# Issuing the loads of modulation weights that go with interleaved steps from GpSimd's queue

## The chip, the cores and the metric

The kernel runs on one core of a Trainium2 chip. The metric is the device time of one launch in microseconds; lower is better. The engines of a core work side by side, each through its own queue in order: TensorE (PE) for matrix products, VectorE (DVE), ScalarE (ACT) and GpSimd (POOL) for the rest, and SyncE (SP), which here only issues loads and stores.

## The reference, cut to what matters

Two stacks of blocks run over one sequence of 512 tokens of width 1024, in 32-bit floats. The change touches the second stack only. There, each of two layers is modulated by a vector `c`:

```
c_act = silu(c)
for i in range(2):
    mod = c_act @ ada_w[i] + ada_b[i]          # [1024] x [1024, 6144]
    sh1, sc1, g1, sh2, sc2, g2 = split(mod, 6)
    h = rmsnorm(x, g[i, 0]) * (1 + sc1) + sh1
    y = mlstm(h) if i == 0 else sgu(h)         # sgu: the gated mixer
    x = x + g1 * rmsnorm(y, g[i, 1])
    h = rmsnorm(x, g[i, 2]) * (1 + sc2) + sh2
    y = square(relu(h @ w1[i])) @ w2[i]        # the feed-forward part, hidden width 4096
    x = x + g2 * rmsnorm(y, g[i, 3])
return x
```

`ada_w` is `ada_w_2` in the kernel. Each of the twelve parts of the two products `c_act @ ada_w[i]` needs 4 MB of weights and next to no arithmetic.

## The kernel before

All large products run on TensorE as three products of split operands: a weight piece of 256 rows and 512 columns (512 KB) is loaded by SyncE (L210 in `w_piece`, L391 in `seven`, which forms products of blocks with fewer multiplications), ScalarE writes its high part (L191) and VectorE the rest (L192); TensorE then runs the products of lines 287 to 289. The raw piece and both parts lie in slots of one pool, `mid`, which are taken again in the order in which they come free. In the mixer there are eleven such slots for weights.

The modulation products run on VectorE. A part of 1024 columns is summed in 16 steps, eight row blocks times two halves of 512 columns. A load of 128 x 512 values (256 KB, L562) brings the weights into one of two buffers, taken in turn (`ada_in`); the step multiplies them by one column of `c_act` and adds them to an accumulator (L571 for the first two steps, L573 after that). A load is put in the program one step ahead: step i issues load i+1. Load i+1 writes the buffer that step i-1 has read.

Where `ada_sum` has no `then`, all 16 steps stand in the program in one place: three parts in the first stack's first mixer and two in the mlstm. Where it has one, the steps go to a list, `ada_steps`, and `dense` takes `ada_rate` of them (two or three) ahead of each weight piece. That is so for the feed-forward part of layer 0 (its own part 5, and parts 0 and 1 of layer 1), for the gated mixer `sgu` (parts 3, 4 and 2 of layer 1; the last with an empty function) and for the feed-forward part of layer 1 (part 5).

The order in which each engine gets its instructions is planned ahead, by readiness and program order, and is fixed when the kernel runs; so a step can stand earlier or later than the program puts it. The planner also sets the waits.

GpSimd has other work: the differences of weight blocks in `seven` (lines 411, 415, 420 and 425), the addition of a bias in the gated mixer (L1558), sums of blocks (lines 363 and 367), and the reciprocal root of every norm (L480). It issues no load.

Of the kernel before, what the change touches and what calls it, by code (L numbers as in the profile page):

```python
# [16 lines left out]
P = 128  # L17
# [13 lines left out]
def kernel(ctx: ExitStack, tc: tile.TileContext, inp: dict, out: bass.AP):  # L31
    nc = tc.nc
    V, S, G, T = nc.vector, nc.scalar, nc.gpsimd, nc.tensor
# [520 lines left out]
    def ada_sum(l, part, then=None):  # L554


        ts = []

        def load(i):
            ts.append(ada_in[0].next())  # L560
            c0 = part * D + (i % 2) * 512
            nc.sync.dma_start(ts[i], inp["ada_w_2"][l, i // 2 * P : (i // 2 + 1) * P, c0 : c0 + 512])  # L562

        def step(i):
            if i == 0:
                load(0)
            if i < 2 * KD - 1:
                load(i + 1)
            a, t, ck = ada_acc[i % 2], ts[i], c_act[:, i // 2 : i // 2 + 1]
            if i < 2:  # L570
                V.tensor_scalar(a, t, ck, None, op0=mult)  # L571
            else:
                V.scalar_tensor_tensor(a, t, ck, a, op0=mult, op1=add)  # L573

        steps = [lambda i=i: step(i) for i in range(2 * KD)]
        if then:
            ada_steps.extend((*steps, lambda: None, then, lambda: None, lambda: None))
        else:
            for f in steps:
                f()  # L580
# [1065 lines left out]
```

## Time and profile before

| | |
|---|---|
| median of 3 runs | 2264.4 us (2262.87 to 2268.69) |
| the profiled execution's own time | 2268.93 us |
| its span, first to last instruction | 2266.9 us |
| TensorE busy | 2215.9 us, 98% |
| VectorE busy | 1471.9 us, 65% |
| ScalarE busy | 975.1 us, 43% |
| GpSimd busy | 239.2 us, 11% |
| loads of modulation weights | 192, 256 KB each |

The rows further down come from one execution. Times are microseconds from the start of the span, unless a row says ns. SPq is SyncE's queue, POOL is GpSimd. The second stack's feed-forward part of layer 0 runs from about 1230 to 1590, the gated mixer from about 1590 to 1900, the last feed-forward part after that. A wait is put down to what came last of all that an instruction waited for.

### The profile page before, as it was taken

The numbers are of one execution on the slowest core, as the hardware profiler recorded it, in microseconds if no ns is written. First come the engines' busy times: TensorE is split into PE (matmuls) and PEld (weight loads), VectorE is DVE, ScalarE is ACT, GpSimd is POOL, SyncE is SP. The second block draws the span as 40 slices with busy tenths as digits, with TensorE's granted clock in tenths as the row PEclk, the third lists the DMA queues.
The fourth block names the chain that finished last, engine by engine and source line by source line (L and its number), as shares of the span: only waits on it lengthen the run. The fifth ranks groups of instructions, "written<-read, shape, count | busy, mean of one in ns | idle before, by whom it ended". The sixth has DMA issues, their size and how long they took to land.

```text
span 2266.9 us, 29330 instructions
## 1 busy us (share of the span) xinstructions
PE 2215.9 (98%) x11112; PEld 1820.6 (80%) x11112; DVE 1471.9 (65%) x2610; ACT 975.1 (43%) x1784; POOL 239.2 (11%) x209
## 2 busy tenths in 40 slices
PE   8999999999999999999999999999999899999998
PEld 6787888787778777887777888988777787898996
DVE  5665755844995857843647847867667748655765
ACT  4333344424344544343444534525434335443543
POOL 0000000100000000000211131221002200131130
PEclk9999999999999999999999999999999999999999
DMA  5343424222222124223414435352344434323322
GB/s 166 120 125 108 151 85 122 98 71 66 84 75 75 38 88 142 91 71 115 141 61 131 154 111 167 103 177 87 113 154 149 141 133 139 104 85 101 119 93 77
DMA packets 158062, 251.16 MB, mean 111 GB/s; under 512 B 13785, under 2 KB 59057, under 8 KB 157921
## 3 DMA queue, kind: packets, MB, share of 16 engines
q1 hardware_dynamic: 157920, 249.29, 34.8%
q8 instruction: 87, 1.43, 0.3%
q14 instruction: 55, 0.44, 0.1%
HBM read 247.15 MB, written 2.10 MB: 110 GB/s over the span
## 4 chain that ended last, share of the span: by engine, by line
PE 76%; DVE 10%; DMA 7%; ACT 3%; issue 3%; POOL 1%; SPq 0%; DVEq 0%; POOLq 0%; ACTq 0%
PE bank L287 23%; PE bank L288 23%; PE bank L289 23%; DMA small<-in_ada_w_dram 4%; DVE mid L192 3%; DVE small L573 2%; PE bank L1109 2%; PE bank L294 1%; ACT mid L191 1%; POOL tiny_c L480 1%; PE bank L1124 1%; PE bank L1308 1%; PE bank L1293 1%; DMA mid<-in_b_w_in_dram 1%; DVE x_res L642 0%
## 5 line engine op out<-in xcount | busy, mean ns | idle before, releaser
L192 DVE TENSOR_TENSOR mid<-mid,mid 128x512 fp32r<-128x512 f32 (+2 forms) x530 | 512.9, 989 | 443.1 <-ACT mid L191 278.1
L191 ACT CAST mid<-mid 128x512 fp32r<-128x512 f32 (+2 forms) x530 | 419.6, 818 | 761.0 <-DMA mid<-in_ffn_w_dram 138.6
L287 PE MATMUL bank<-mid,mid 128*128 128x512 f32 (+1 forms) x1320 | 492.8, 373 | 7.5 <-ACT small L1567 4.4
L288 PE MATMUL bank<-mid,mid 128*128 128x512 f32 (+1 forms) x1320 | 489.8, 371 | 1.5 <-DVE mid L192 1.5
L289 PE MATMUL bank<-mid,mid 128*128 128x512 f32 (+1 forms) x1320 | 489.2, 371 | 0.0
L287 PE MATMUL bank<-xt_hi,mid 128*128 128x512 f32 (+1 forms) x1216 | 426.9, 352 | 11.7 <-ACT small L1567 5.8
L289 PE MATMUL bank<-xt_hi,mid 128*128 128x512 f32 (+1 forms) x1216 | 425.1, 350 | 1.3 <-DVE mid L192 1.3
L288 PE MATMUL bank<-xt_lo,mid 128*128 128x512 f32 (+1 forms) x1216 | 424.7, 349 | 0.0
L287 PEld LDWEIGHTS bank<-mid,mid 128*128 128x128 f32 x1320 | 248.9, 189 | 56.3 <-ACT small L1567 4.8
L288 PEld LDWEIGHTS bank<-mid,mid 128*128 128x128 f32 x1320 | 248.7, 188 | 46.0 <-DVE mid L192 2.1
L289 PEld LDWEIGHTS bank<-mid,mid 128*128 128x128 f32 x1320 | 248.7, 188 | 45.3
L287 PEld LDWEIGHTS bank<-xt_hi,mid 128*128 128x128 f32 x1216 | 229.4, 189 | 48.3 <-ACT small L1567 6.7
L289 PEld LDWEIGHTS bank<-xt_hi,mid 128*128 128x128 f32 x1216 | 229.6, 189 | 32.7 <-DVE mid L192 1.5
L288 PEld LDWEIGHTS bank<-xt_lo,mid 128*128 128x128 f32 x1216 | 229.8, 189 | 31.9 <-issue 1.3
L287 PE MATMUL bank<-mid,xt_hi 128*128 128x512 f32 (+1 forms) x640 | 252.7, 395 | 0.0
L288 PE MATMUL bank<-mid,xt_hi 128*128 128x512 f32 (+1 forms) x640 | 250.2, 391 | 0.0
L289 PE MATMUL bank<-mid,xt_lo 128*128 128x512 f32 (+1 forms) x640 | 250.1, 391 | 0.0
L573 DVE SCALAR_TENSOR_TENSOR small<-small,c_act,small 128x512 f32<-128x512 f32 x168 | 132.5, 804 | 78.6 <-DMA small<-in_ada_w_dram 77.9
L289 PEld LDWEIGHTS bank<-mid,xt_lo 128*128 128x128 f32 x640 | 120.5, 188 | 26.6
L288 PEld LDWEIGHTS bank<-mid,xt_hi 128*128 128x128 f32 x640 | 120.6, 188 | 25.5 <-DVE mid L192 0.3
L287 PEld LDWEIGHTS bank<-mid,xt_hi 128*128 128x128 f32 x640 | 120.7, 189 | 24.9
L480 POOL TENSOR_TENSOR tiny_c<-tiny_c,minus_half 128x1 f32<-128x1 f32 (+1 forms) x68 | 52.3, 773 | 747.5 <-DVE tiny_c L494 375.5
(297 smaller groups left out, 2305.0 us busy)
## 6 DMA issues: line engine op xcount, KB each, us to landing
mid<-in_ffn_w_dram SPq DMA_DIRECT2D x128, 512.0 KB, 3.7
small<-in_ada_w_dram SPq DMA_DIRECT2D x192, 256.0 KB, 2.9
mid<-in_dsa_w_in_dram SPq DMA_DIRECT2D x36, 512.0 KB, 3.5
mid<-in_gla_w_in_dram SPq DMA_DIRECT2D x32, 512.0 KB, 4.4
mid<-in_b_w_in_dram SPq DMA_DIRECT2D x32, 512.0 KB, 3.6
mid<-in_a_w_in_dram SPq DMA_DIRECT2D x24, 512.0 KB, 3.8
mid<-in_gla_w_in_dram SPq DMA_DIRECT2D x32, 256.0 KB, 3.0
mid<-in_gla_w_out_dram SPq DMA_DIRECT2D x16, 512.0 KB, 3.7
```

The source lines that it names most:

```text
L191: S.copy(hi, src)
L192: V.tensor_sub(lo, src, hi.bitcast(F32))
L287: T.matmul(o, lhsT=lh, rhs=rh, start=start, stop=False)
L288: T.matmul(o, lhsT=lh, rhs=rl, start=False, stop=False)
L289: turns.passed(o, T.matmul(o, lhsT=ll, rhs=rh, start=False, stop=stop))
L294: i = T.transpose(b[:, blk(c)], src, ident)
L480: G.tensor_tensor(r, v, minus_half[:, 0:m], op=ALU.pow)
L573: V.scalar_tensor_tensor(a, t, ck, a, op0=mult, op1=add)
L1109: T.matmul(b[:, :n], lhsT=QT[tb][:, blk(c)], rhs=KT[:, :n], start=True, stop=True)
L1124: T.transpose(b[:, blk(c)], es[c][:, blk(j)], ident)
L1293: T.matmul(sb[:, :n], lhsT=KT[pr, c // 2, blk(j)], rhs=QT[pr, c // 2, j * P :], start=True, stop=True)
L1308: T.matmul(nb[i // 2][:, (i % 2) * 129 : (i % 2) * 129 + 129], lhsT=Dm[j][:, blk(i - j)], rhs=vv[j][:, c, :], start=j == 0, stop=j == i)
```

## The change

The loads of those sums whose steps go to the list are issued by GpSimd (`G` is `nc.gpsimd`); the others are issued by SyncE as before. Buffers, steps and arithmetic are the same.

```
         def load(i):
             ts.append(ada_in[0].next())
             c0 = part * D + (i % 2) * 512
-            nc.sync.dma_start(ts[i], inp["ada_w_2"][l, i // 2 * P : (i // 2 + 1) * P, c0 : c0 + 512])
+            (G if then else nc.sync).dma_start(ts[i], inp["ada_w_2"][l, i // 2 * P : (i // 2 + 1) * P, c0 : c0 + 512])
```

## Rows read from the trace of the kernel before

**Rows 1.** The page, first part: busy us, share of the span, instructions.
```profile
PE 2215.9 (98%) x11112; PEld 1820.6 (80%) x11112; DVE 1471.9 (65%) x2610; ACT 975.1 (43%) x1784; POOL 239.2 (11%) x209
```
**Rows 2.** Stretches: length, busy us of each engine (instructions), clock, DMA share, GB/s.
```profile
1385.00:1430.00 45.00, 43.38 (x207) 35.76 (x207) 29.09 (x35) 9.43 (x10) 9.97 (x4) 1.00 0.54 174
...
1670.00:1800.00 130.00, 118.88 (x545) 96.96 (x544) 97.82 (x133) 47.15 (x65) 29.07 (x22) 0.95 0.52 164
...
1930.00:2267.00 337.00, 328.65 (x1936) 288.32 (x1935) 203.71 (x208) 145.12 (x200) 67.47 (x29) 1.00 0.30 97
```
**Rows 3.** The chain by line: 1200-1240, 1240-1300, 1385-1430, 1470-1510, 1670-1800, 1870-1930.
```profile
by line: DMA small<-in_ada_w_dram 20.8%; DVE small L573 15.9%; DVE x_res L642 9.1%; issue 7.5%; POOL tiny_c L480 7.5%; DVE mid L192 5.7%; DVE small L1372 5.4%; DVE xt_lo L192 4.6%; ACT junk L486 4.2%; DVE small L520 3.0%; DVE small L519 3.0
...
by line: DVE mid L192 18.3%; issue 16.2%; DMA small<-in_ada_w_dram 9.0%; PE bank L289 6.3%; PE bank L287 6.2%; PE bank L288 5.5%; DVE small L573 4.1%; POOL tiny_c L480 3.2%; PE bank L294 2.9%; DVE x_res L642 2.6%; DVE small L617 2.3%; DVE m
...
by line: DMA small<-in_ada_w_dram 49.6%; DVE small L573 19.2%; DVE mid L192 6.2%; issue 4.9%; PE bank L287 4.2%; DVE small L1455 4.2%; PE bank L289 3.4%; PE bank L288 3.4%; DVE tiny_c L589 2.7%; SPq L391 1.0%; DVE small L571 0.9%; SPq L562 
...
by line: DMA small<-in_ada_w_dram 27.1%; PE bank L287 18.6%; PE bank L288 17.5%; PE bank L289 17.4%; DVE mid L192 7.4%; DVE small L573 5.5%; issue 2.6%; DVE small L1455 1.5%; DVE tiny_c L589 1.5%; DVE small L571 1.0%; DVE tiny_c L599 0.2%; 
...
by line: DMA small<-in_ada_w_dram 18.8%; PE bank L287 12.7%; PE bank L288 11.9%; PE bank L289 11.6%; DMA mid<-in_b_w_in_dram 7.4%; DVE mid L192 7.3%; DVE small L573 5.5%; issue 3.3%; DMA mid<-in_b_w_out_dram 2.9%; ACT mid L191 2.8%; DMA sma
...
by line: DMA small<-in_ada_w_dram 13.8%; DVE mid L192 10.7%; DVE small L573 10.6%; issue 9.7%; POOL tiny_c L480 8.6%; DVE small L1369 6.6%; DVE x_res L642 6.2%; DVE xt_lo L192 4.4%; DVE small L627 3.6%; PE bank L287 3.4%; DVE small L520 3.0
```
**Rows 4.** Pieces of the chain, 1385 to 1425: start, us, what.
```profile
1387.53 4.93 DMA small<-in_ada_w_dram
...
1392.55 0.76 DVE small L573
1393.33 2.85 DMA small<-in_ada_w_dram
...
1409.92 4.88 DMA small<-in_ada_w_dram
```
**Rows 5.** VectorE's waits, 1200 to 1930: us in total, times, longest.
```profile
DVE small L573 <- DMA small<-in_ada_w_dram: 63.6, 43, 4.6
```
**Rows 6.** SyncE's timeline in the mixer: start, us of the run, issues.
```profile
1714.35 2.45 SPq L562 DMA_DIRECT2D small<-in_ada_w_dram  x2
...
1748.55 1.62 SPq L562 DMA_DIRECT2D small<-in_ada_w_dram  x2
...
1781.29 4.16 SPq L562 DMA_DIRECT2D small<-in_ada_w_dram  x3
```
**Rows 7.** Weight pieces in the chain, 1670 to 1800.
```profile
1716.89 3.86 DMA mid<-in_b_w_in_dram
...
1750.26 5.76 DMA mid<-in_b_w_in_dram
...
1785.50 3.71 DMA mid<-in_b_w_out_dram
```
**Rows 8.** TensorE's waits, 1670 to 1800.
```profile
PE bank L287 <- ACT small L1567: 10.2, 3, 4.4
```
**Rows 9.** VectorE's timeline, 1730 to 1800: two steps.
```profile
1752.31 0.75 DVE L573 SCALAR_TENSOR_TENSOR small<-small,c_act,small 128x512 f32<-128x512 f32 x1 [2.49 <-DMA small<-in_ada_w_dram]
...
1786.14 0.75 DVE L573 SCALAR_TENSOR_TENSOR small<-small,c_act,small 128x512 f32<-128x512 f32 x1
```
**Rows 10.** The changed line, 1200 to 1930: ns of an issue min/median/max; landing.
```profile
L562 SPq DMA_DIRECT2D small<-in_ada_w_dram x110: 327/328/456, 1202.0 to 1912.2; - x110
...
DMA to landing us min/median/max: 2.7/2.9/6.3
```
**Rows 11.** GpSimd's groups, 1200 to 1930: busy us, mean ns, idle before.
```profile
L1558 POOL TENSOR_TENSOR mid<-mid,small 128x512 f32<-128x512 f32 x16 | 28.7, 1814 | 72.7 <-DVE mid L1557 72.7
...
L425 POOL TENSOR_TENSOR mid<-mid,mid 128x1024 f32<-128x1024 f32 x6 | 14.5, 2410 | 17.9 <-issue 17.9
```
**Rows 12.** GpSimd's timeline, 1690 to 1730: one instruction, idle before it in brackets.
```profile
1695.94 1.06 POOL L501 TENSOR_SCALAR tiny_c<-tiny_c 128x1 f32<-128x1 f32 x1 [85.06 <-DVE tiny_c L500]
```
**Rows 13.** The step's line, 1200 to 1930: ns min/median/max, first and last start.
```profile
L573 DVE SCALAR_TENSOR_TENSOR small<-small,c_act,small x98: 681/751/2889, 1205.2 to 1920.1; 128x512 f32<-128x512 f32 x98
```

More of the change, by code (lines that the diff above doesn't have):

```diff
@@ L561, in load @@
             c0 = part * D + (i % 2) * 512
-            nc.sync.dma_start(ts[i], inp["ada_w_2"][l, i // 2 * P : (i // 2 + 1) * P, c0 : c0 + 512])
+            (G if then else nc.sync).dma_start(ts[i], inp["ada_w_2"][l, i // 2 * P : (i // 2 + 1) * P, c0 : c0 + 512])
         def step(i):
```

## The prediction

> **What bounds the kernel now.** The page was read first: TensorE is busy for nearly the whole span [rows 1], so a change that only moves loads can win no more than TensorE's gaps in the stretches where those loads run, and what it can lose has no such limit. The stretches come next [rows 2]. From 1385 to 1430 us (the first down-projection of the first feed-forward part) TensorE is busy 43.38 of 45 us; from 1670 to 1800 (the gated mixer) 118.88 of 130, at a granted clock of 0.95 of full speed, which lies between its two levels of 1.2 and 2.4 GHz; from 1930 to the end no load of the changed line is left. The 11.1 us of gap and the lower clock (5 in 100 of 118.88, 5.9 us) are what there is to win in the mixer.
>
> The chain of work that ended last says what fills the gaps [rows 3]. In six stretches a large share of it is the loading of modulation weights: 20.8% of 40 us, 9.0% of 60, 49.6% of 45, 27.1% of 40, 18.8% of 130 and 13.8% of 60, which is 8.3 + 5.4 + 22.3 + 10.8 + 24.4 + 8.3 = 79.5 us. The pieces of the chain show the pattern [rows 4]: a load of 2.9 to 4.9 us, a VectorE step of 0.76 us, the next load within 0.1 us. There are 3, 2, 6, 3, 7 and 3 such pieces in the stretches, 24 in all, 3.31 us each. The reason is the ring of two buffers: load i+1 writes the buffer that step i-1 reads, so it is issued when that step ends, and VectorE, whose queue is in order, stands at step i+1 until it has landed. VectorE waited so 43 times for 63.6 us between 1200 and 1930 [rows 5]. SyncE is not late for these loads: it issues them the moment the step ends. It is late for the weight pieces queued behind them [rows 6].
>
> **The change part by part.** *How many.* The sums with a step after them are those of the first feed-forward part (parts 5 of layer 0, 0 and 1 of layer 1), of the mixer (3, 4, 2; the empty lambda of part 2 counts too) and of the second feed-forward part (5): seven sums of 16 loads, 112 of 192. All 24 trips of the chain are theirs. The loads, the buffers and the steps stay; the queue changes, and with it who stands behind whom.
>
> *Removed: weight pieces standing behind modulation loads in SyncE's queue.* In the mixer the chain has three weight pieces [rows 7]; each was issued within 0.1 us of the end of a run of modulation loads [rows 6]: 1714.35 + 2.45 = 1716.80 against 1716.89, 1748.55 + 1.62 = 1750.17 against 1750.26, 1781.29 + 4.16 = 1785.45 against 1785.50. TensorE's three waits for the gelu that is queued behind their splits cost 10.2 us [rows 8]. Issued earlier, the second piece would gain at most until VectorE's own last step there, 1752.31 + 0.75 = 1753.06 against a landing at 1756.02: 3.0 us; the third 1786.89 against 1789.21: 2.3 us [rows 7, 9]; the first gets a third of the 10.2, 3.4. That is 8.7; I take 7, as a piece also needs a free slot. Bounds: 0, and 10.2 + 5.9 of clock = 16.
>
> *Moved: the issue itself.* SyncE's issue takes 0.33 us and the load lands 2.9 us after its start (median) [rows 10]. The trace has no load issued by GpSimd. From below it costs 0.33, as now; from above 2.4, as a GpSimd operation on 1024 elements [rows 11]. The nearest row is a GpSimd instruction on one element per partition that comes after idle, 1.06 us [rows 12]: almost nothing to move, so it is the engine's own cost. I take 1.0, which is 0.67 more for each trip: 24 x 0.67 = 16 us. Nothing hides it, because VectorE already waits in each of the 24. Bounds: 0 and 24 x 2.07 = 50. The Trainium skill speaks against the change here: "DMA: Bandwidth & Descriptors", Latency and other measured facts, has the first byte about 0.4 us later from GpSimd than from SyncE. By that estimate the term would be some 10 us instead of 16; no run here shows it yet.
>
> *Own queue.* The long trips, 4.93 and 4.88 us [rows 4], have a weight piece in the same queue ahead of them. If all 24 took the shortest, 2.7 [rows 10], that would be 79.5 - 64.8 = 15 us less. Both queues still share the same engines, so I take a third, 5 us (bounds 0 and 15).
>
> *Past GpSimd's queue.* Between 1385 and 1430 GpSimd has 10 us of other work [rows 2], four differences of 2.4 us each and more for the next product [rows 11]; a load whose buffer comes free during one stands for the rest of it, and a difference behind a load that waits for VectorE stands too, and with it the split that ScalarE makes of it. In the mixer the additions (1.8 us, 16 of them [rows 11]) wait for VectorE, and loads stand behind those. At the part boundaries the reciprocal root of a norm can stand behind an issue of 1.0 us. Worst in a down-projection would be all 10 us; two of them and the mixer's 16 x 1.8 = 29 give a bound of 49; below it is 0, where the planned order keeps them apart. I take 6: half a difference twice in each of two down-projections (4.8), and one issue ahead of one root (1.0).
>
> *Sum:* 16 + 6 - 7 - 5 = +10 us on the profiled execution's own 2268.93: 2278.9. That execution is 4.5 us above the median of the runs shown, so as a median 2274.4; I say 2274.
>
> **The rivals.** *The loads come no later (faster).* If GpSimd's issue costs no more than SyncE's, the 16 fall away and the conflicts shrink to about 2: 2 - 7 - 5 = -10, a median of 2254. For it speaks that SyncE's queue is really held up [rows 6] and that GpSimd idles most of the span [rows 1]; against it that its smallest instruction takes three times an issue of SyncE [rows 10, 12]. It decides from 0.25 us: (7 + 5 - 6)/24 is the added time for a trip at which the sum is nil. The Trainium skill's fit in "DMA: Bandwidth & Descriptors", Anatomy of one DMA, 2.0 us and the bytes over 436 GB/s, gives 2.6 us for these 256 KB from GpSimd, an estimate below the 2.9 of the row; by it each trip would shrink by 0.3 and the result be on this side, some 17 us below the profiled execution (24 x 0.3 = 7, and the 10 above).
>
> *The order is planned anew (same).* The program's order on each engine is made ahead, and steps were pulled forward over other work (the second feed-forward part's are over by 1930). A plan that knows the loads to be later puts splits in front of the steps, and the longer trips fall where VectorE had idle time: 97.82 of 130 us are busy in the mixer [rows 2]. Then +16 becomes about +8, and the sum +2: 2266. Against it: VectorE waited for loads 43 times under the present plan too.
>
> *GpSimd is held up while VectorE works (much slower).* A VectorE step took 2.889 us at the longest where 0.751 is usual [rows 13], beside GpSimd's differences. If issuing a load suffers in the same way, each trip gains about 2 us: 48 + 6 - 12 = +42, a median of 2306. Against it: an issue need not read a tile. The Trainium skill, "SBUF — State Buffer", the section SBUF: two separate sides, has GpSimd shut out from writing descriptors while VectorE runs in its two-port mode; by that rule the time would come out here, if the steps ran in that mode; no run here shows yet whether they do.
>
> **How the numbers follow.** 0.3% of the median is 6.8 us, about what a measurement of this kernel can tell from none. The forecast, +3 to +22, gets 0.42, of which 0.09 lies within 0.3%. The much slower case gets 0.10, the new plan 0.22, the faster case 0.26, of which 0.04 lies within 0.3%. Slower: 0.33 + 0.10 = 0.43. Same: 0.09 + 0.22 + 0.04 = 0.35. Faster: 0.22. The range has to reach into the cases of both signs: its low end is the faster case's 2254 (0.12 lies below), its high end 2298, where an added 1.6 us for each trip would stand (0.08 above). The forecast's own range is 2267 to 2286.
>
> **What would show it.** In the changed kernel's profile a second queue carries 29 MB (112 x 256 KB); the issue rows give the time to landing, which I expect at 3.3 to 3.9 us against 2.9; VectorE's waits for these loads grow from 63.6 us towards 90; SyncE's weight pieces in the mixer leave earlier and TensorE's wait for the gelu shrinks; in the down-projections TensorE's gap grows from 1.6 us to several. Wrong would be the whole of it if the landing time stayed at 2.9 or less, or if VectorE's waits grew while TensorE's gaps did not.

## The result and the profile after

The changed kernel takes 2302.45 us (median of 4 runs, 2297.8 to 2307.21), the kernel before 2266.06 in the same session: ratio 1.0156 (95% interval 1.0135 to 1.0178), 36 us slower. The prediction was 2274, with a range from 2254 to 2298. The direction was right, the size too small.

The profiled execution of the changed kernel took 2307.21 us, the longest of its four (TensorE's granted clock was 0.86 of full speed between 550 and 600 us, where nothing is changed), so only the stretches of the change are read in it. First the page: the span, busy time by engine, and the queues (packets, MB, share of 16 engines).

```profile
span 2305.4 us, 29370 instructions
...
PE 2229.8 (97%) x11112; PEld 1828.3 (79%) x11112; DVE 1472.0 (64%) x2610; ACT 976.4 (42%) x1784; POOL 298.7 (13%) x321
...
q1 hardware_dynamic: 141792, 219.92, 30.2%
q0 software_dynamic: 8960, 29.37, 4.0%
```

VectorE does what it did in [rows 1]; GpSimd has 112 instructions and 59.5 us more, which is 0.53 us for each of the 112 issues; the second queue carries the forecast 29 MB. The changed line and its landing time, 1200 to 1960 us, against [rows 10]:

```profile
L562 POOL DMA_DIRECT2D small<-in_ada_w_dram x110: 536/538/1212, 1209.0 to 1951.4; - x110
...
DMA to landing us min/median/max: 2.9/3.2/6.6
```

An issue takes 0.54 us and not the 1.0 that I took; landing takes 3.2 us instead of 2.9. A third part is seen only in the chain (1400 to 1426 us), against [rows 4]:

```profile
1409.23 0.76 DVE small L573
1409.99 0.28 issue
1410.27 4.01 DMA small<-in_ada_w_dram
```

From the end of a step to the start of the issue it is 0.28 us; SyncE needed 0.02 (1393.33 after 1392.55 + 0.76 in [rows 4]). VectorE's and TensorE's waits answer to [rows 5] and [rows 8] (1200 to 1960, and the mixer, which now lies from 1695 to 1830: us in total, times, longest):

```profile
DVE small L573 <- DMA small<-in_ada_w_dram: 87.4, 52, 4.2
```
```profile
PE bank L287 <- ACT small L1567: 15.7, 3, 7.4
```

The first is the 90 that was forecast from 63.6. The second was to shrink from 10.2 and grew. The stretches (busy us and count of PE, PEld, DVE, ACT, POOL, then PE's granted clock, DMA share, GB/s), against [rows 2]:

```profile
1400.00:1450.00 50.00, 45.27 (x214) 37.27 (x213) 30.11 (x36) 10.28 (x11) 18.72 (x20) 0.97 0.50 156
1500.00:1520.00 20.00, 14.72 (x55) 11.61 (x54) 12.47 (x16) 2.78 (x3) 5.33 (x9) 0.83 0.50 161
1695.00:1830.00 135.00, 118.29 (x551) 96.62 (x550) 98.42 (x134) 48.21 (x66) 44.16 (x54) 0.95 0.50 158
```

TensorE's gap in the first down-projection is 4.7 us instead of 1.6, a second of 5.3 us comes between 1500 and 1520, and the mixer has 16.7 us where it had 11.1. A gap costs more than its length. The second stretch in pieces of 5 us shows it:

```profile
1505.00:1510.00 5.00, 1.99 (x9) 1.31 (x7) 2.64 (x3) 1.01 (x1) 1.08 (x2) 1.00 0.56 169
1510.00:1515.00 5.00, 2.74 (x7) 2.19 (x8) 3.23 (x6) 1.05 (x1) 1.07 (x2) 0.51 0.51 170
```

TensorE stands still for 3 of the first 5 us, and then the granted clock is 0.51 of full speed, which is the lower of its two levels (1.2 of 2.4 GHz); from 1515 to 1520 it is 0.81 on average, and from 1520 on 1.00.

Why the gelu is late shows in the mixer's timelines, 1765 to 1790: VectorE's, then ScalarE's (start, us, instruction, idle before it and what ended it).

```profile
1775.67 0.75 DVE L573 SCALAR_TENSOR_TENSOR small<-small,c_act,small 128x512 f32<-128x512 f32 x1 [3.30 <-DMA small<-in_ada_w_dram]
1778.39 0.75 DVE L573 SCALAR_TENSOR_TENSOR small<-small,c_act,small 128x512 f32<-128x512 f32 x1 [1.97 <-DMA small<-in_ada_w_dram]
...
1782.53 0.75 DVE L573 SCALAR_TENSOR_TENSOR small<-small,c_act,small 128x512 f32<-128x512 f32 x1 [0.99 <-DMA small<-in_ada_w_dram]
1783.20 0.68 DVE L1573 TENSOR_TENSOR small<-small,small 128x512 f32<-128x512 f32 x1
```
```profile
1783.92 0.62 ACT L191 CAST mid<-small 128x512 fp32r<-128x512 f32 x1 [13.09 <-DVE small L1573]
1784.44 1.04 ACT L191 CAST mid<-mid 128x1024 fp32r<-128x1024 f32 x1
1785.71 0.69 ACT L1567 ACTIVATE small<-bank,vec 128x512 f32<-128x512 f32 x1 [0.23 <-DVE mid L192]
```

The product that ScalarE is to split (L1573) stands on VectorE behind steps that wait for their loads; ScalarE waits 13.09 us for it, and the gelu (L1567), for which TensorE waits, stands behind that split. The split of a weight piece between them (1784.44) waits for nothing. The same place in the kernel before, ScalarE's timeline from 1745 to 1760:

```profile
1756.10 1.04 ACT L191 CAST mid<-mid 128x1024 fp32r<-128x1024 f32 x1 [4.29 <-DMA mid<-in_b_w_in_dram]
1757.05 1.13 ACT L191 CAST mid<-small 128x512 fp32r<-128x512 f32 x2
1758.42 0.69 ACT L1567 ACTIVATE small<-bank,vec 128x512 f32<-128x512 f32 x1 [0.24 <-DVE mid L192]
```

There it was a weight piece that ScalarE waited for, 4.29 us. That wait is gone in the changed kernel, and a longer one for VectorE stands in its place.

### The profile page after: what moved, and what is told of

The parts are those of the page before. It is cut to its first block, busy times and chain, and to the rows that moved or that the text cites. A ratio compares the mean times of both kernels' runs of the same rounds, so it can differ in the third digit from the quotient of the medians.

```text
span 2305.4 us, 29370 instructions
## 1 busy us (share of the span) xinstructions
PE 2229.8 (97%) x11112; PEld 1828.3 (79%) x11112; DVE 1472.0 (64%) x2610; ACT 976.4 (42%) x1784; POOL 298.7 (13%) x321
## 4 chain that ended last, share of the span: by engine, by line
PE 68%; issue 11%; DVE 8%; DMA 7%; ACT 2%; POOL 2%; SPq 0%; POOLq 0%; DVEq 0%; ACTq 0%
PE bank L287 20%; PE bank L288 20%; PE bank L289 20%; DMA small<-in_ada_w_dram 5%; DVE mid L192 3%; DVE small L573 2%; PE bank L1109 2%; PE bank L294 1%; ACT mid L191 1%; POOL tiny_c L480 1%; PE bank L1124 1%; DMA mid<-in_ffn_w_dram 1%; PE bank L1308 1%; PE bank L1293 1%; POOL mid L1558 1%
## 5 line engine op out<-in xcount | busy, mean ns | idle before, releaser
L480 POOL TENSOR_TENSOR tiny_c<-tiny_c,minus_half 128x1 f32<-128x1 f32 (+1 forms) x68 | 52.5, 774 | 601.2 <-DVE tiny_c L494 373.8
```

What stands on the lines that cost most here:

```text
L480: G.tensor_tensor(r, v, minus_half[:, 0:m], op=ALU.pow)
```

## The experiments

They ran in later sessions, in which the kernel before took 2271 to 2275 us (median); so the ratios to it are compared, or medians of one call.

**A second queue by itself, and the three places.** The condition of line 562 in the changed kernel is cut to one load, or to the sums of one part:

```
-            (G if then else nc.sync).dma_start(ts[i], ...)
+            (G if then and (l, part, i) == (0, 5, 0) else nc.sync).dma_start(ts[i], ...)
```

> One single load of the 112 goes to GpSimd's queue (the first of the first feed-forward part's first sum); the other 111 stay with SyncE. Order of TensorE, VectorE and ScalarE as before. Theory 'the second queue has a price of its own at the end': in the changed kernel 8.5 us passed from the last VectorE addition to the end of the span where 3.0 passed before, with nothing running that the trace shows; one load is enough to bring these 5.5 us: 2271.6, a ratio of 1.0024. Rival 'every trip costs the same': 36.4 us over the 24 trips that stood on the chain is 1.5 us each, so one load costs 0 to 1.5 us: 2266 to 2267.6.

> Only the first feed-forward part's three sums (48 loads) go to GpSimd's queue. Theory 'place decides' (the loss is where GpSimd has other work in its queue, and there is the price at the end): by the landmarks of the two traces, 21 us up to the end of this part's last down-projection, and 5.5 at the end: +26.5, 2292.5, ratio 1.0117. Rival 'every trip costs the same': 14 of the 24 trips at 1.5 us, +21, 2287, and no more time at the end than before.

> Only the gated mixer's three sums (48 loads) go to GpSimd's queue. Theory 'place decides': the landmarks give 4.5 us across the mixer, and 5.5 at the end: +10, 2276, ratio 1.0044. Rival 'every trip costs the same': 7 of 24 trips at 1.5 us, +10.6, 2276.7, but all of it in the mixer and nothing at the end. The two differ in where the time is, not in the total.

> Only the second feed-forward part's one sum (16 loads) goes to GpSimd's queue. Theory 'place decides': the landmarks give 3 us at the boundary where these loads are, and 5.5 at the end: +8.5, 2274.5, ratio 1.0038. Rival 'every trip costs the same': 3 of 24 trips at 1.5 us, +4.6, 2270.6, ratio 1.0020.

Measured: one load 0.9996 (0.9979 to 1.0012), the first feed-forward part 1.0056 (1.0040 to 1.0073), the mixer 1.0071 (1.0043 to 1.0099), the second feed-forward part 1.0010 (0.9991 to 1.0030). With one load the end is as before: my theory of it fell in this form, and comes back below. The three sum to 1.37% of 1.56%. In these three the plan moves too (42 to 50 of VectorE's 2610 instructions stand at another place than before, 134 in the changed kernel). My split by place was wrong: the first part cost 13 us and not 26.5 (nor the rival's 21), the second part 2 and not 8.5. The mixer's sums cost 16 us, 10 to 22; the 10 that both sides expected lie at the edge of that. They start long before the mixer. In GpSimd's timeline of that run, 1475 to 1560, they sit in the down-projections of the part before:

```profile
1503.49 0.54 POOL L562 DMA_DIRECT2D small<-in_ada_w_dram  x1 [2.41 <-DVE small L573]
1505.88 0.54 POOL L562 DMA_DIRECT2D small<-in_ada_w_dram  x1 [1.86 <-DVE small L573]
1506.44 2.40 POOL L411 TENSOR_TENSOR mid<-mid,mid 128x1024 f32<-128x1024 f32 x1
```

The same row of the kernel before:

```profile
1493.89 2.43 POOL L411 TENSOR_TENSOR mid<-mid,mid 128x1024 f32<-128x1024 f32 x1 [41.76 <-DMA mid<-in_ffn_w_dram]
```

Before, the difference began when its weight piece landed, after 41.76 us of idle time. Now the loads, each of which waits for a step of VectorE, are ahead of it, and it begins 12.6 us later. Only 7.8 us of that are the loads: one of its two pieces lands at 1498.61, as the chain of that run has it. TensorE did not wait for this difference. Its one long wait in the same stretch (1470 to 1560) ends when ScalarE has split that piece; SyncE had waited 5.2 us for TensorE to free a slot before it issued it:

```profile
1494.15 4.46 DMA mid<-in_ffn_w_dram
```
```profile
PE bank L287 <- ACT mid L191: 5.4, 1, 5.4
```

So the row shows that loads hold up a difference, and not what this costs.

**The planned order apart from the queue.** The program is planned twice. The order of one plan is put on the other, engine by engine, by order-only dependencies; only the loads find their own place:

```
+    _, order = traced("gpsimd")        # the plan of the changed kernel
+    nc, _ = traced("sync", order)      # SyncE issues, the other engines in that order
```

The second run exchanges the two names.

> The loads are issued by SyncE as before, but VectorE, ScalarE, TensorE and GpSimd (and SyncE's other transfers) have their instructions in the order that was planned for the changed kernel. Theory 'GpSimd's queue is in order' (differences stand behind loads that wait for VectorE, and loads behind differences): the new plan alone costs little, ratio 0.999 to 1.004. Rival 'the new plan is the cause': all of the loss is here, ratio about 1.0156. Rival 'longer trips': 1.000.

> The 112 loads are issued by GpSimd, but VectorE, ScalarE, TensorE, GpSimd's other work and SyncE's other transfers keep the order that was planned for the kernel before; only the loads' own places in GpSimd's queue are new. Theory 'GpSimd's queue is in order': the loss stays, ratio 1.010 to 1.018. Rival 'the new plan is the cause': ratio 1.000 to 1.003. Rival 'longer trips': the loss stays too, and is seen as longer times to landing and not as differences that start late.

Measured: 1.0018 (1.0005 to 1.0032), 4 us; and 1.0138 (1.0116 to 1.0160), 31 us. The plan is a small part; the rest comes with GpSimd's queue. In the second run ScalarE waits longer for the differences of line 411 (1400 to 1530, and the kernel before from 1390 to 1515):

```profile
ACT mid L191 <- POOL mid L411: 14.3, 3, 8.3
```
```profile
ACT mid L191 <- POOL mid L411: 4.2, 3, 1.8
```

**GpSimd's other work out of the queue.** VectorE makes the differences of the seven products, the two of their left side, and the mixer's additions, in both runs of this pair (and in every run that follows but the last):

```
-        G.tensor_tensor(b12, b12, b11, op=sub)
+        V.tensor_tensor(b12, b12, b11, op=sub)
...
-                G.tensor_add(v, v, br)
+                V.tensor_add(v, v, br)
```

> The control for the next run: the loads by SyncE, and VectorE makes the differences of the seven products, the two of their left side and the additions of the mixer, which GpSimd made. Slower than before, as VectorE gets some 67 us of work in stretches where TensorE sometimes waits for it: ratio 1.005 to 1.03. All theories say the same of it.

> As the run before, on VectorE the differences and additions, but the 112 loads by GpSimd, everything else in the order of the run before. GpSimd then has next to nothing but loads. Theory 'GpSimd's queue is in order': only the longer trips are left, 0.3 us (3.2 to landing against 2.9) for 24 of them, 7 us or 0.3%, against the run before; most of the 36 us is gone. Rival 'longer trips': the whole loss of 1.2 to 1.6% against the run before. Rival 'the new plan is the cause': none, 0.0%.

Measured: 0.9894 (0.9868 to 0.9920) with SyncE, 0.9998 (0.9979 to 1.0017) with GpSimd; medians 2251.99 and 2272.36. Two misses. The control is no slower but 20 to 24 us faster than the kernel before (by medians and by ratio), and the queue still costs 20 to 24 us without the differences in it. The first lines of the control's page begin:

```profile
PE 2212.1 (98%) x11112; PEld 1819.2 (81%) x11112; DVE 1471.6 (65%) x2678; ACT 973.8 (43%) x1784; POOL 77.6 (3%) x141
```

The 68 instructions that GpSimd gives up add nothing to VectorE's busy time: 1471.6 us with them, 1471.9 without [rows 1]. They had made VectorE's own work longer: the longest step was 2889 ns [rows 13], and is 777 now:

```profile
L573 DVE SCALAR_TENSOR_TENSOR small<-small,c_act,small x168: 681/747/777, 47.4 to 1907.5; 128x512 f32<-128x512 f32 x168
```

With it TensorE's wait for the gelu falls from 10.2 us [rows 8] to 2.4, though SyncE still issues these loads. Most of what the control gains lies there, in the mixer, where it is the additions of L1558 that moved: from 1700 to 1850 TensorE's gap is 2.5 us where it was 10.2, and the granted clock 0.99 where it was 0.95.

The chains of the pair at the first boundary show what is left, SyncE's first:

```profile
1210.98 0.76 DVE small L573
1211.74 0.02 issue
1211.76 2.78 DMA small<-in_ada_w_dram
...
1214.63 0.77 DVE small L573
```
```profile
1217.10 0.77 DVE small L573
1217.87 0.28 issue
1218.15 3.08 DMA small<-in_ada_w_dram
...
1221.33 0.76 DVE small L573
...
1226.67 0.54 POOL small L562
1227.20 0.02 issue
1227.22 0.58 POOL tiny_c L480
```

From one step to the next but one it is 3.65 us with SyncE (then 3.77) and 4.23 with GpSimd (then 4.29). And an issue stands ahead of a root (L480).

**The roots out of the queue as well.** The roots (L480, L501 with its addition) become VectorE's reciprocal, in both runs; the output is another one:

```
-        G.tensor_tensor(r, v, minus_half[:, 0:m], op=ALU.pow)
+        V.reciprocal(r, v)
```

> The control for the next run: as the run with VectorE's differences and SyncE's loads, and the reciprocal roots of the norms, the last other work of GpSimd in these stretches, are replaced by VectorE's reciprocal, so the output is another one; only the time is read. Both theories: somewhat faster than 0.989 of the kernel before, 0.980 to 0.988, as a norm no longer goes through a second engine.

> As the run before, with the reciprocals on VectorE (another output), but the 112 loads by GpSimd, everything else in the order of the run before. In the stretches of these sums GpSimd has nothing but loads. With the roots on GpSimd the same exchange cost 20 us (0.9%). Theory 'longer trips' (two steps took 4.25 us instead of 3.77 at the part's boundary, and there VectorE waits for nearly every load): most of the 20 us stays, 0.7 to 1.0% against the run before, and it arises at the two boundaries. Rival 'roots stand behind loads in GpSimd's queue': 0.0 to 0.3%.

Measured: 0.9838 (0.9794 to 0.9881) and 0.9916 (0.9883 to 0.9949), medians 2239.93 and 2255.75: 16 us, and some 5 to 30 by the bounds of the two ratios. Every run of the second was slower than every run of the first, by 8 us at least. Counted by the n-th matrix instruction of either trace, TensorE falls back by 15 us between 1190 and 1950, at the two boundaries, in the down-projections and in the mixer. So a cost of this size stays where GpSimd has nothing but loads in these stretches. VectorE's waits for them are 53.5 us in the one and 84.5 in the other (1200 to 1960).

**A third buffer.** The ring gets a third buffer (room for it comes from other small tiles, in both runs), and step i loads i + 2:

```
-            if i < 2 * KD - 1:
-                load(i + 1)
+            for j in range(0 if i == 0 else i + 2, min(i + 3, 2 * KD)):
+                load(j)
```

> The faster version so far (VectorE makes the differences, SyncE issues) with three buffers for these loads, two of them ahead of the step. Theory 'trips': three steps take one trip and one step, (3.02 + 0.75) / 3 = 1.26 us each instead of 1.89, where VectorE waits for every load; VectorE's waits of 67.4 us shrink to some 30, and the time goes from 0.989 to 0.982 to 0.987 of the kernel before. Rival 'VectorE's waits cost nothing outside of the boundaries' : 0.987 to 0.990.

> As the run before with three buffers, but the 112 loads by GpSimd, everything else in the order of the run before. Theory 'trips': the longer trip is spread over three steps instead of two, so the 20 us that the exchange cost with two buffers become at most 13, and less where a load now lands before its step. Rival 'roots stand behind loads in GpSimd's queue': the 20 us stay, as the queue holds as many loads as before.

Measured: 0.9892 (0.9855 to 0.9929) and 0.9947 (0.9926 to 0.9967), medians 2252.72 and 2262.88. The exchange costs 10 us instead of 20, as the theory of trips has it. With SyncE the third buffer halves VectorE's waits (55.1 to 28.7 us, 1200 to 1960) and no gain is seen (0.9892 against 0.9894; the bounds still allow the upper end of the 0.982 to 0.987 that was expected): there the rival fits better, these waits had cover. So a trip has no fixed price for each microsecond: shorter ones won nothing here, longer ones cost.

**A longer trip without GpSimd, and a queue without GpSimd.** Two halves of each load on SyncE; and the 112 loads on ScalarE (`nc.scalar.dma_start`), both against the run with SyncE and VectorE's differences:

```
+            for a, b in ((0, 64), (64, P)):
+                nc.sync.dma_start(ts[i][a:b, :], src[a:b, :])
```

> As the run with VectorE's differences and SyncE's loads, everything in its order, but each of the 112 loads is issued by SyncE as two halves of 64 partitions, so that a load costs two issues. A longer trip with no other queue and no GpSimd in it. Theory 'longer trips': GpSimd's trip is 0.55 us longer (0.28 instead of 0.02 from the end of the step to the issue, 3.1 to 3.3 instead of 2.85 to landing) and costs 16 us without the roots; two issues make it 0.33 longer, which is 16 x 0.33 / 0.55 = 10 us, 0.4% against the run with one issue. Rival 'it is GpSimd and not the trip': 0.0 to 0.1%.

> As the run with VectorE's differences and SyncE's loads, everything else in its order, but the 112 loads are issued by ScalarE, so that they have a queue of their own, and the weight pieces no longer stand behind them in SyncE's. Theory of the prediction 'own queue' (7 us from weight pieces that leave earlier, 5 from loads without a piece ahead): up to 12 us faster than the run with SyncE, if ScalarE's own work costs nothing. Rival 'the weight pieces wait for slots, and no queue makes them earlier': no gain, and 0 to 20 us slower, as copies now stand behind loads that wait for VectorE.

Measured: two issues 1.0064 (1.0041 to 1.0088), which is 1.7% over the run with one issue; ScalarE 0.9913 (0.9886 to 0.9939) against 0.9894. A longer trip costs without any GpSimd in it. The size was a miss: each half took 0.47 to 0.51 us to issue and not 0.33, so two steps took 4.1 to 4.4 us, as with GpSimd, and the cost was not 10 us but 36 to 38. The weight pieces stand in the same queue there; how much of it is theirs is not separated. The queue of its own on ScalarE, on the other hand, with weight pieces free of loads, gains nothing. That alone does not show that the pieces' freedom is worth nothing: ScalarE's splits stand behind the loads there, and only 2.4 us of waiting for the gelu were left to win.

**The end.** From the end of GpSimd's last root to the end of the span, by the traces:

| run | loads on GpSimd | us |
|---|---|---|
| kernel before | 0 | 4.4 |
| one load; second part; first part; mixer | 1; 16; 48; 48 | 4.6; 4.5; 5.0; 4.9 |
| changed kernel; old plan; VectorE's differences; three buffers | 112 | 10.0 each |

Only the run without roots has 112 loads and no long end: 3.4 us from VectorE's last addition, where the changed kernel has 8.5. Two more runs. In the first, loads on GpSimd and reciprocals on VectorE as above, the last four roots are GpSimd's again (`QUEUE[1:]` holds something for them only); the second is the changed kernel with all 192 loads on GpSimd:

```
+        G.tensor_tensor(r, v, minus_half[:, 0:m], op=ALU.pow) if QUEUE[1:] else V.reciprocal(r, v)
...
-            (G if then else nc.sync).dma_start(ts[i], ...)
+            G.dma_start(ts[i], ...)
```

> As the run without roots and with the loads by GpSimd (reciprocals on VectorE, another output), but the four roots of the very last norms are GpSimd's again, in the last 40 us, long after its last load. Theory 'GpSimd has something to close at the end for every load it issued, and can only begin after its last instruction': with 112 loads 10.0 us passed from the end of the last root to the end of the span, with 48 loads 4.9 to 5.0, with none 4.4 to 4.5; without roots at the end it was hidden (3.4 us from VectorE's last addition to the end). So here 10.0 us from the last root again, and 8.5 us from the last addition. Rival 'it is of the whole program and not of the last instruction', or a chance of the profiled executions: 3 to 3.5 us from the last addition, as in the run without roots.

> The changed kernel with all 192 loads of the line on GpSimd's queue. Theory 'something to close for every load': by the points 48 loads 5.0 us and 112 loads 10.0 us (0.08 us a load, 1.2 besides) the end of the last root to the end of the span takes 16 us. Rival 'a fixed price': 10.0 us.

Measured, the first run (2257.41 us): the last root, and the head of the answer with the span.

```profile
core 0 of [0], span 2255.7 us
...
2244.41 0.93 POOL L480 TENSOR_TENSOR tiny_c<-tiny_c,minus_half 128x1 f32<-128x1 f32 x1 [4.66 <-DVE tiny_c L492]
```

2255.7 - 2245.3 = 10.4 us: the long end counts from GpSimd's last instruction, and four roots, more than 300 us after the last load, uncover it. Without them it passes unseen. The count of loads does not set it: with 192 loads (2335.44 us against 2273.7 of the kernel before) it was 8.3 us, neither 16 nor 10.0. Both were run once. After the last addition and the last store the traces show no instruction; what the time is and what sets its length stay open.

## Why the prediction was wrong

The sum was 16 + 6 - 7 - 5 = +10. The runs make it, of 36:

- **The trip (+16): right in size, in part by luck.** The pair without roots gives 16 us, with wide bounds (5 to 30). Its make-up was not the issue of 1.0 us: the issue takes 0.54, but it starts 0.26 us later and the landing takes 0.3 longer, 0.55 us for each of 24 trips, 13 us. That is read at the first boundary; over all loads of the pair with VectorE's differences the median landing is 3.4 us with SyncE and 3.3 with GpSimd. And the prediction's "nothing hides it" does not hold as a price for each microsecond, as the third buffer shows. The Trainium skill, "DMA: Bandwidth & Descriptors", Latency and other measured facts, has the first byte 0.4 us later from GpSimd; the 0.3 of landing is close to that. The Trainium skill's fit on that page, in Anatomy of one DMA, is further off: 2.6 us by estimate, 3.2 measured.
- **Past GpSimd's queue (+6): too small.** 31 us with the old plan less 20 to 24 without the differences and additions is 7 to 11 us, some 10. I priced loads that stand behind half a difference. The other direction, a difference behind loads that wait for VectorE, I named and gave no price; it was 7.8 us in the row above, and ScalarE's wait for these differences grew from 4.2 to 14.3 us. How much of that reaches TensorE, and by which path, is not followed.
- **The two credits (-7, -5): the step that failed.** The -7 came from weight pieces late behind loads, and the gelu late behind them [rows 6 to 8]. In the kernel before that is so (4.29 us above, ahead of one of the three waits). But I let VectorE's times stand while its trips grew: in the changed kernel the piece is there in time, the product that is split ahead of the gelu comes later, ScalarE waits 13.09 us for it, and the wait for the gelu rose from 10.2 to 15.7 us. With SyncE's queue unchanged and GpSimd's work on VectorE it fell to 2.4; with the loads on GpSimd as well it was 2.7. So what was left to win lay with VectorE. The -5 was for long trips that a queue of their own would shorten. They stayed long: 4.01 us in the chain above, 6.6 at most where it had been 6.3.
- **Not in the sum at all:** 5.5 us at the end (10.0 instead of 4.4 after the last root), and 4 us (1 to 7) of the new plan.

16 + 10 + 5.5 + 4 = 35.5 of the measured 36 us. The terms are each known to some microseconds only, so that they meet the total this closely is luck too. Against the forecast that is 12 for the credits, 4 for the queue and 9.5 for what was left out. (In the two traces TensorE falls back by 26 us between 1190 and 1950, and the end is 5.5 us longer.)

Of the rivals, *the loads come no later* is out: trips grew by 0.55 us, over its bound of 0.25. *The order is planned anew* happened, but the new order costs 4 us and hides nothing. *GpSimd is held up while VectorE works* gave the nearest time, 2306, by a mechanism that did not act: 78 of the 112 issues ran mostly beside a VectorE instruction, and their median is 538 ns, as that of the other 34; the longest took 1.2 us. Of what would show it, the second queue, VectorE's waits and the down-projection's gaps came; landing at 3.2 lay just under the 3.3 to 3.9; the weight pieces came earlier, and the wait for the gelu grew all the same.

The faster runs point the other way: leave the loads with SyncE and take the elementwise work from GpSimd, 0.9894 of the kernel before.

## What to carry to other kernels

A queue is free only if nothing else in it waits: before a transfer is moved to an engine, list what that engine does in order, and what each transfer waits for. Where buffers are so few that each load waits for the step before the last, price the whole trip (end of the step, start of the issue, landing) and not only the issue. A credit for work that is issued earlier has to be read from the engine that waits for it, back along its own queue, before it enters a sum.

## What the runs showed of the hardware that was not expected

- GpSimd's elementwise work took as much from VectorE as it did for it: 68 instructions moved, and VectorE's busy time went from 1471.9 to 1471.6 us. The Trainium skill, "SBUF — State Buffer", the section SBUF: two separate sides, has a GpSimd operation and a VectorE operation with two SBUF inputs shut each other out for a whole instruction; the steps' longest time, 2889 ns beside GpSimd's differences and 777 without, agrees: all eight steps over 1.0 us in the kernel before ran beside a difference or an addition on GpSimd.
- The Trainium skill, in the same section, has GpSimd unable to write descriptors in VectorE's two-port mode. No run here shows that: the issues beside VectorE's work took 538 ns (median), as the others did.
- From the end of GpSimd's last instruction to the end of the span 10.0 to 10.4 us passed where it had issued 112 loads, 4.9 to 5.0 with 48, 4.4 to 4.6 with 0 to 16, and 8.3 with 192; it passed unseen where its last instruction was early.
- A GpSimd issue starts 0.26 to 0.28 us after the event that it waits for, SyncE's after 0.02.
